# Strassen's scheme for the last two up tiles of each MLP's first block, with the operand sums made behind its first four tiles

## The chip, the cores and the metric

The kernel runs on one core of a Trainium2 chip. The metric is the device time of one execution in microseconds (us); a comparison takes the median of several runs. TensorE (PE) multiplies, VectorE (DVE) and ScalarE (ACT) do elementwise work, GpSimd (POOL) a little of it, and SyncE (SP) issues nearly all transfers.

## The reference, cut to what matters

Four layers run over 512 tokens of width 1024. Each has a mixer (retention, convolution, gated linear attention, retention) and then a squared-ReLU MLP of inner width 4096, with an RMS norm ahead of and behind each part:

```python
def sq_relu_mlp(u, w_up, w_down):
    return jnp.square(jax.nn.relu(u @ w_up)) @ w_down

u = rmsnorm(h, norm_gains[i, 2])
h = h + rmsnorm(sq_relu_mlp(u, mlp_w_up[i], mlp_w_down[i]), norm_gains[i, 3])
```

All of it is float32. The change touches `u @ w_up` alone.

## The kernel before, in words

Everything is stored with features on the 128 partitions and the 512 tokens along the row, so an activation of width 1024 is eight tiles of 128x512. Each float32 operand is cut into a high part (rounded by an ACT copy, L146 or L190 for weights, L435 or L437 for activations) and a low part (the rest, a DVE subtraction, L147, L191, L442, L444), and a product is three matmuls: high by high, high by low, low by high (`mm3`, L454 to L456). PE's order is the order in which the program is written. The order on ACT, DVE and SP is set by a planner that runs through the program with estimated times: an engine that comes free takes, of the instructions whose inputs and buffers are ready by its reckoning, the one that was written first. On the chip each engine then keeps that order.

Weights come as panels of 128x1024 (eight 128x128 blocks, the whole inner width for one output tile). `Stream` loads a panel into a raw buffer and cuts it into a ring of six high and six low buffers. It runs some panels ahead of the matmuls.

An MLP (`mlp`, L683 on) works through four blocks of 1024 inner features: first eight up tiles, each evacuated into `act` by `up` (a ReLU times the norm's factor `r` on DVE, L705; a square on ACT, L706; the two parts on ACT and DVE), and then eight down tiles that add into `y`. Blocks 1 to 3 form the up tiles in pairs with one level of Strassen's scheme (`seven`): a pair is a 2x2 product of halves (four of the eight inner tiles, 256 of the 512 tokens, one of the two output tiles), and takes seven products of 4 x 3 matmuls of 256 columns instead of two tiles of 8 x 3 matmuls of 512. The products are written in the order 1, 2, 5, 6, 4, 3, 7 and use three PSUM banks: `a` for products 1, 6 and 7, `bd` for 2 and 4, `c` for 5 and 3. Two temporaries `e1` and `e2` hold the partial sums that ACT copies out of `a` and `c`. The weight sums that it needs are formed by `pair` (four DVE operations of 128x512, L195 to L200, and three and a half panels cut instead of two). The activation sums (products 3, 5, 6 and 7) are formed once in an MLP by `make(k)`, k from 0 to 3: two ACT scalings (L613, L614), four DVE operations of 128x256 (L615 to L618), and two splits (L435 and L442, tile `wS`). Before the change this is written behind down tiles 2 to 5 of block 0.

Block 0 is formed without the scheme. At the start of an MLP the norm's factor `r` is not known yet, and the second half of the tokens still comes out of the mixer's closing. So `lead` forms up tiles 0 to 3 together, first for tokens 0 to 255 and then for the rest, and keeps their four banks. It then has `norm` write the sum of squares' mean (`mean2`, two matmuls, L285) and the steps to `r` (ACT L461, DVE L467 to L469) into the program once 11.0 us of matmuls, by the program's own count, have gone by after the four tiles. Right behind this it writes the evacuation of the four tiles and of those finished meanwhile. PSUM has eight banks here: seven with the tag `ps` that matmul results share, and one, `st`, for the mean. The temporaries `tmp` (128x512) have four buffers. `make`, `up`, `seven` and the steps to `r` all draw on them.

Of the kernel before, what the change touches and what calls it, by code (L numbers as in the profile page):

```python
# [23 lines left out]
T = 512  # L24
D = 1024
KD = D // P
# [213 lines left out]
def _spare(pool, tag, bufs, w=8 * P):  # L240

    def alloc():
        return [[pool.tile([P, w], F32R, name=f"w{tag}", tag=tag, bufs=bufs) for _ in range(8 * P // w)] for _ in range(2)]
    return alloc
# [98 lines left out]
class Kern:  # L343
# [339 lines left out]
    def mlp(self, close, early=()):  # L683
        nc = self.nc
        FB = 4
        early = list(early)

        def step():

            if early:  # L690
                self.W.cut_early(early.pop(0))

        with self.tc.tile_pool(name="mlp", bufs=1) as mp:
            self.W.keep(FB * 2 * KD - 4, [_spare(mp, "w", 8)] * 4)
            for b in range(1, FB):
                for n in range(0, KD, 2):
                    self.W.pairs[self.W.at + b * 2 * KD + n] = mp
            make = self.combos(mp)
            for b in range(FB):
                act = [self.pair(mp, "act", 2 * KD) for _ in range(KD)]  # L700

                def up(n, ps, c, t=None):
                    lo, hi = c
                    t = self.tmp() if t is None else t
                    nc.vector.scalar_tensor_tensor(t[:, lo:hi], ps[:, lo:hi], 0.0, self.r[:, lo:hi], ALU.max, ALU.mult)  # L705
                    nc.scalar.activation(t[:, lo:hi], t[:, lo:hi], AF.Square)  # L706
                    self.split(act[n], t[:, lo:hi], c)

                n0 = 0
                if b == 0:  # L710
                    n0 = 4
                    self.lead(n0, up)
                if b:
                    for n in range(0, KD, 2):
                        self.seven(lambda i, t: up(n + i, t, (0, T), t))
                    n0 = KD
                for n in range(n0, KD):
                    ps = self.proj()
                    self.when(lambda n=n, ps=ps: up(n, ps, (0, T)))

                def down(n, ps, c):
                    if b == 0:
                        close.first(n, ps)
                    else:
                        close.add(n, ps, c)

                n1 = KD - 4 if b == FB - 1 else KD
                def complete(n, ps):
                    down(n, ps, (0, T))
                    step()  # L730
                    if b == FB - 1:
                        close.done(n)


                for n, ps in enumerate(self.proj2(act)):
                    complete(n, ps)
                for n in range(2, n1):
                    complete(n, self.proj(act))
                    if b == 0 and n < 6:
                        make(n - 2)  # L740
                if n1 < KD:
                    pan = self.W.group(4, 4)
                    self.trail([([pan[i].blk(k) for k in range(KD)], act, n1 + i) for i in range(4)], down, close)
# [1006 lines left out]
```

## Time and profile before

| | us |
|---|---|
| median of 3 runs | 2722.18 (2721.29 to 2722.32) |
| the profiled execution | 2721.62 |
| its span | 2719.9 |
| PE busy | 2671.6 (98%) |
| DVE busy | 1939.8 (71%) |
| ACT busy | 1348.7 (50%) |

The profile is of one execution. The span runs from its first to its last instruction. A matmul's shown duration includes its passage through the array, so the next one starts long before the shown end; what a stream of matmuls costs is the step from one start to the next.

### The profile page before, as it was taken

The page shows a single profiled execution, that of the slowest core. Times are in us where ns is not written, and L with a number is a line of the kernel's source. Part 1 is how long each engine was busy: PE and PEld are TensorE (multiplying, and loading weights), DVE is VectorE, ACT ScalarE, POOL GpSimd, SP SyncE. Part 2 cuts the span into 40 slices and gives each one's busy share as a digit, 9 for nine tenths or more (in the row PEclk, how much of TensorE's full clock was granted, in tenths as well). Part 3 has the DMA queues.
Part 4 walks back from the last instruction along what each step waited for, and adds up shares of the span by engine and source line. Part 5 has one row for each costly group of instructions (what it writes and reads, how often), then busy time and mean ns, then how long its engine had stood idle before and what let it go on. Part 6 is the DMA issues. An engine that isn't in the chain of part 4 may idle for free.

```text
span 2719.9 us, 38414 instructions
## 1 busy us (share of the span) xinstructions
PE 2671.6 (98%) x15232; PEld 2349.5 (86%) x15232; DVE 1939.8 (71%) x3022; ACT 1348.7 (50%) x2098; POOL 180.8 (7%) x183
## 2 busy tenths in 40 slices
PE   9999999999999899999999999999999999999998
PEld 7888889889998898999887888899888888989997
DVE  8755568878859977766788686777765565777766
ACT  5443445655536455544477555455544443555432
POOL 5320000000008400000000000000000000000000
PEclk9999999999999999999999999999999999999999
DMA  5433232676636432332222232333223222223322
GB/s 188 168 132 100 71 100 82 244 268 233 218 124 212 144 112 86 109 117 65 91 70 78 71 109 70 109 109 109 93 63 93 85 70 85 86 86 109 117 63 70
DMA packets 89029, 313.37 MB, mean 115 GB/s; under 512 B 9872, under 2 KB 12176, under 8 KB 88848
## 3 DMA queue, kind: packets, MB, share of 16 engines
q1 hardware_dynamic: 85536, 299.31, 34.4%
q0 software_dynamic: 3168, 11.54, 1.1%
q8 instruction: 119, 1.95, 0.3%
q14 instruction: 62, 0.51, 0.1%
q10 hardware_dynamic: 144, 0.07, 0.0%
HBM read 271.55 MB, written 39.32 MB: 114 GB/s over the span
## 4 chain that ended last, share of the span: by engine, by line
PE 84%; DVE 8%; DMA 3%; ACT 3%; POOL 1%; issue 1%; SPq 0%; DVEq 0%; ACTq 0%
PE ps L455 28%; PE ps L456 28%; PE ps L454 28%; DVE wlo L147 1%; DMA wraw<-in_wst_dram 1%; DMA cuth<-whi 1%; DVE ps L1098 1%; DVE acc L267 1%; ACT whi L146 1%; DVE tmp L329 0%; DMA cutl<-wlo 0%; DVE h L332 0%; PE st L275 0%; DMA h<-in_xT_dram 0%; DVE actl L442 0%
## 5 line engine op out<-in xcount | busy, mean ns | idle before, releaser
L454 PE MATMUL ps<-xh,whi 128*128 128x256 f32 (+1 forms) x1920 | 643.7, 335 | 0.9 <-ACT xh L437 0.9
L455 PE MATMUL ps<-xl,whi 128*128 128x256 f32 (+1 forms) x1920 | 640.1, 333 | 1.1 <-DVE xl L444 1.1
L456 PE MATMUL ps<-xh,wlo 128*128 128x256 f32 (+1 forms) x1920 | 639.5, 333 | 0.0
L146 ACT ACTIVATE whi<-wraw 128x1024 fp32r<-128x1024 f32 (+1 forms) x300 | 312.2, 1045 | 315.2 <-PE ps L455 213.6
L147 DVE TENSOR_TENSOR wlo<-wraw,whi 128x1024 fp32r<-128x1024 f32 (+1 forms) x300 | 365.1, 1220 | 107.5 <-ACT whi L146 105.0
L455 PEld LDWEIGHTS ps<-xl,whi 128*128 128x128 f32 x1920 | 365.3, 190 | 38.7 <-DVE xl L444 1.5
L454 PEld LDWEIGHTS ps<-xh,whi 128*128 128x128 f32 x1920 | 365.2, 190 | 38.1 <-ACT xh L437 1.1
L456 PEld LDWEIGHTS ps<-xh,wlo 128*128 128x128 f32 x1920 | 365.1, 190 | 35.7
L455 PE MATMUL ps<-actl,whi 128*128 128x512 f32 x896 | 350.3, 391 | 3.7 <-DVE actl L442 3.7
L454 PE MATMUL ps<-acth,whi 128*128 128x512 f32 x896 | 349.0, 390 | 0.6 <-ACT acth L435 0.5
L456 PE MATMUL ps<-acth,wlo 128*128 128x512 f32 x896 | 348.7, 389 | 0.0
L308 DVE TENSOR_TENSOR y<-y,ps 128x512 f32<-128x512 f32 (+1 forms) x200 | 114.8, 579 | 216.0 <-PE ps L456 215.3
L454 PE MATMUL ps<-wS,whi 128*128 128x256 f32 x768 | 217.5, 283 | 0.7 <-ACT tmp L654 0.7
L456 PE MATMUL ps<-wS,wlo 128*128 128x256 f32 x768 | 217.3, 283 | 0.0
L455 PE MATMUL ps<-wS,whi 128*128 128x256 f32 x768 | 217.3, 283 | 0.0
L455 PEld LDWEIGHTS ps<-actl,whi 128*128 128x128 f32 x896 | 168.2, 188 | 43.7 <-DVE actl L442 9.4
L454 PEld LDWEIGHTS ps<-acth,whi 128*128 128x128 f32 x896 | 168.2, 188 | 35.9 <-ACT acth L435 1.4
L456 PEld LDWEIGHTS ps<-acth,wlo 128*128 128x128 f32 x896 | 168.2, 188 | 34.6
L190 ACT ACTIVATE whi<-wraw 128x1024 fp32r<-128x1024 f32 x96 | 101.4, 1057 | 142.0 <-PE ps L455 115.6
L190 ACT ACTIVATE whi<-raw 128x1024 fp32r<-128x1024 f32 x96 | 81.2, 845 | 160.0 <-PE ps L455 130.0
L267 DVE TENSOR_TENSOR acc<-acc,sq 128x256 f32<-128x256 f32 (+1 forms) x246 | 121.8, 498 | 51.1 <-ACT sq L266 44.8
L454 PEld LDWEIGHTS ps<-wS,whi 128*128 128x128 f32 x768 | 147.4, 192 | 1.1 <-ACT tmp L654 1.1
(345 smaller groups left out, 5249.0 us busy)
## 6 DMA issues: line engine op xcount, KB each, us to landing
wraw<-in_wst_dram SPq DMA_DIRECT2D x390, 512.0 KB, 3.7
raw<-in_wst_dram SPq DMA_DIRECT2D x48, 512.0 KB, 4.3
cuth<-whi SPq DMA_DIRECT2D x24, 512.0 KB, 3.5
cutl<-wlo SPq DMA_DIRECT2D x24, 512.0 KB, 4.1
whi<-cuth SPq DMA_DIRECT2D x20, 512.0 KB, 3.7
wlo<-cutl SPq DMA_DIRECT2D x20, 512.0 KB, 4.6
diagh<-dg POOLq DMA_DIRECT2D x11, 512.0 KB, 3.2
diagl<-dg POOLq DMA_DIRECT2D x11, 512.0 KB, 3.6
```

Source lines behind the costliest of these rows:

```text
L146: nc.scalar.activation(h, raw[:, c:d], AF.Copy)
L147: nc.vector.tensor_tensor(l, raw[:, c:d], h.bitcast(F32), ALU.subtract)
L190: nc.scalar.activation(hi[0][:, :w], raw[:, :w], AF.Copy)
L267: nc.vector.tensor_tensor(acc, acc, t, ALU.add)
L308: self.K.nc.vector.tensor_tensor(y, y, ps[:, a:b], ALU.add)
L454: mm(out, lhsT=A[0], rhs=B[0], start=start, stop=False)
L455: mm(out, lhsT=A[0], rhs=B[1], start=False, stop=False)
L456: mm(out, lhsT=A[1], rhs=B[0], start=False, stop=stop)
L1098: nc.vector.scalar_tensor_tensor(sums[i], x, w, sums[i], ALU.mult, ALU.add)
```

## The change

The up tiles 6 and 7 of block 0 are formed by `seven` as one pair; tiles 4 and 5 stay as they were. `pair` builds the weight sums for it. The four `make(k)` are written right behind `lead`, ahead of tiles 4 and 5, instead of behind down tiles 2 to 5. Tiles 0 to 3 and blocks 1 to 3 stay. The assertion checks at build time that the pair's panels haven't been loaded as plain ones.

```diff
-            for b in range(1, FB):
-                for n in range(0, KD, 2):
+            for b in range(FB):
+                for n in range(0 if b else KD - 2, KD, 2):
+                    assert self.W.at + b * 2 * KD + n >= self.W.loaded
                     self.W.pairs[self.W.at + b * 2 * KD + n] = mp
...
                 if b == 0:
                     n0 = 4
                     self.lead(n0, up)
-                if b:
-                    for n in range(0, KD, 2):
-                        self.seven(lambda i, t: up(n + i, t, (0, T), t))
-                    n0 = KD
-                for n in range(n0, KD):
-                    ps = self.proj()
-                    self.when(lambda n=n, ps=ps: up(n, ps, (0, T)))
+                    for k in range(4):
+                        make(k)
+                    for n in range(n0, KD - 2):
+                        ps = self.proj()
+                        self.when(lambda n=n, ps=ps: up(n, ps, (0, T)))
+                for n in range(0 if b else KD - 2, KD, 2):
+                    self.seven(lambda i, t: up(n + i, t, (0, T), t))
...
                     complete(n, self.proj(act))
-                    if b == 0 and n < 6:
-                        make(n - 2)
```

## Rows read from the trace of the kernel before

**Rows 1.** The page: span, busy time of three engines, the chain's shares by engine

```profile
span 2719.9 us, 38414 instructions
PE 2671.6 (98%) x15232; PEld 2349.5 (86%) x15232; DVE 1939.8 (71%) x3022; ACT 1348.7 (50%) x2098; POOL 180.8 (7%) x183
PE 84%; DVE 8%; DMA 3%; ACT 3%; POOL 1%; issue 1%; SPq 0%; DVEq 0%; ACTq 0%
```

**Rows 2.** Timeline of PE, first MLP: start us, us, engine, line, operation, tiles [idle before]

```profile
460.33 0.40 PE L454 MATMUL ps<-xh,whi 128*128 128x512 f32 x1
...
471.93 0.62 PE L285 MATMUL st<-sq,onesr 128*128 128x512 f32 x2
472.39 0.40 PE L454 MATMUL ps<-xh,whi 128*128 128x512 f32 x1
...
482.62 0.39 PE L454 MATMUL ps<-acth,whi 128*128 128x512 f32 x1
...
486.93 0.50 PE L455 MATMUL ps<-actl,whi 128*128 128x512 f32 x1 [0.24 <-DVE actl L442]
```

**Rows 3.** Windows (span, busy us of PE, PEld, DVE, ACT, POOL, PEclk, DMA): four pairs

```profile
613.53:653.85 40.32, 40.32 (x338) 40.31 (x336) 36.21 (x51) 27.38 (x44) 0.00 (x0) 1.00 0.53 164
```

**Rows 4.** Timeline of ACT and DVE, first MLP, from the mean to the evacuations

```profile
472.59 0.69 ACT L461 ACTIVATE tmp<-st,eps 128x512 f32<-128x512 f32 x1 [0.32 <-PE st L285]
473.45 0.74 DVE L467 SCALAR_TENSOR_TENSOR tmp<-st,eps,tmp 128x512 f32<-128x512 f32 x1
474.95 0.69 DVE L469 SCALAR_TENSOR_TENSOR rx<-tmp 128x512 f32<-128x512 f32 x1
475.68 2.48 DVE L705 SCALAR_TENSOR_TENSOR tmp<-ps,rx 128x512 f32<-128x512 f32 x4
480.85 1.29 DVE L442 TENSOR_TENSOR actl<-tmp,acth 128x512 fp32r<-128x512 f32 x2
```

**Rows 5.** Timelines of PE and DVE, the same places in the last MLP

```profile
2397.86 0.62 PE L285 MATMUL st<-sq,onesr 128*128 128x512 f32 x2
2401.61 2.49 DVE L705 SCALAR_TENSOR_TENSOR tmp<-ps,rx 128x512 f32<-128x512 f32 x4
```

**Rows 6.** Windows up to the first evacuation, first and last MLP

```profile
455.10:475.70 20.60, 20.60 (x113) 17.93 (x113) 15.39 (x26) 10.64 (x18) 0.00 (x0) 1.00 0.45 137
2381.00:2401.60 20.60, 20.60 (x114) 17.93 (x113) 15.39 (x25) 10.75 (x18) 0.00 (x0) 1.00 0.43 139
```

**Rows 7.** DVE's groups by line, 455.1 to 475.6: xcount | busy, mean ns | idle before

```profile
L147 DVE TENSOR_TENSOR wlo<-wraw,whi 128x1024 fp32r<-128x1024 f32 x6 | 7.3, 1222 | 3.7 <-ACT whi L146 3.7
L267 DVE TENSOR_TENSOR acc<-acc,sq 128x256 f32<-128x256 f32 x14 | 5.8, 422 | 0.6
```

**Rows 8.** DVE's groups by line, 486 to 512, for operations of `make`

```profile
L442 DVE TENSOR_TENSOR wS<-tmp,wS 128x512 fp32r<-128x512 f32 x8 | 5.5, 686 | 0.1
L615 DVE TENSOR_TENSOR tmp<-tmp 128x256 f32<-128x256 f32 x4 | 1.7, 422 | 0.2
```

**Rows 9.** Timeline of DVE: steps from start to start for three sizes

```profile
490.64 0.42 DVE L618 TENSOR_TENSOR tmp<-tmp 128x256 f32<-128x256 f32 x1
490.97 0.42 DVE L617 TENSOR_TENSOR tmp<-tmp 128x256 f32<-128x256 f32 x1
...
509.07 1.22 DVE L191 TENSOR_TENSOR wlo<-raw,whi 128x1024 fp32r<-128x1024 f32 x1
510.21 0.69 DVE L442 TENSOR_TENSOR wS<-tmp,wS 128x512 fp32r<-128x512 f32 x1
510.81 0.69 DVE L195 TENSOR_TENSOR wraw<-wraw,raw 128x512 f32<-128x512 f32 x1
```

**Rows 10.** Timeline of PE: a wait in the third layer's mixer

```profile
1574.82 0.38 PE L454 MATMUL ps<-ogh,whi 128*128 128x256 f32 x1 [2.73 <-ACT ogh L435]
1575.63 0.58 PE L455 MATMUL ps<-ogl,whi 128*128 128x256 f32 x1 [0.43 <-DVE ogl L442]
```

**Rows 11.** Windows: the stretch right behind that wait

```profile
1575.60:1579.00 3.40, 3.37 (x16) 3.37 (x16) 1.33 (x2) 0.63 (x1) 0.00 (x0) 0.50 0.38 140
```

## The prediction

> **What bounds the kernel now.** I read the page first: PE is busy for 98% of the span and carries 84% of the chain of work that ended last, DVE 8% [rows 1]. So PE's stream of matmuls sets the time, and a change counts by the matmul time that it removes and by the gaps that it opens in that stream. Then I read PE's timeline through block 0 of the first MLP. Up tiles 4 to 7 run from 460.33 to 482.62 without a gap, with the mean's two matmuls at 471.93 taking 0.46 of it, and the first small waits stand behind them, at the start of the down tiles, for the low parts of `act` (486.93; with the one before it 0.6 us) [rows 2]. Last I followed DVE and ACT over the same stretch: the mean's result leads by ACT 472.59, DVE 473.45 to 474.95 to the first evacuation at 475.68, four of them back to back [rows 4]. The last MLP has the same distances (mean 2397.86, evacuation 2401.61) [rows 5]; so I work out one MLP and multiply by four.
>
> **What the pair saves.** 96 matmuls of 512 columns take 482.62 - 460.33 - 0.46 = 21.83 us, 0.2274 each [rows 2]. Tiles 6 and 7 are 48 of them: 10.92 us. Four pairs by the scheme took 40.32 us [rows 3], 10.08 a pair (84 matmuls at 0.120). Saved: 0.84 us in an MLP, 3.4 us in all. By the Trainium skill ("TensorE: Matmul & The Clock Gate", section Back-to-back issue gap) a lone matmul's step is its columns at the full clock plus 2.5 ns, and the same section warns that weight loads lengthen it at small widths. By the bare formula the pair would save an estimated 1.2 us; the row has the weight loads in it (PEld busy 40.31 of 40.32) and decides.
>
> **The bank that the pair waits for.** This is what the saving has to be held against. There are seven `ps` banks. Tiles 0 to 3 hold four until the first evacuations, tiles 4 and 5 two, so product 1 takes the seventh, and product 2 (`bd`) must wait for the first evacuation. Before, tile 6 filled the seventh bank for 5.5 us, and the mean, `r` and the evacuation ran behind it. Product 1 lasts 1.44 us. Where does the mean stand? The count of 11.0 us passes 10.36 in tiles 4 and 5 and 0.65 in two steps of product 1 (0.33 each by the program's count); they take 0.72 us, so the mean is again issued at about 471.95. PE then does the other half of product 1, until 471.95 + 0.46 + 0.72 = 473.1. The first evacuation starts at 475.68 and ends 0.7 later, at 476.4 [rows 4]. Wait: 3.3 us, with the chain from mean to evacuation exactly as fast as before. It can't be less unless that chain is shorter, and it has one ACT and four DVE operations in a row. Product 5's bank follows 0.6 us after and costs nothing.
>
> **What delays that chain.** DVE has 20.6 us from the last part of x to the first evacuation and is busy for 15.4 of them: 5.2 idle, in the first MLP as in the last [rows 6]. Six panels' low parts are in it [rows 7]. Steps on DVE, start to start: 0.33 us for 128x256, 0.60 for 128x512, 1.14 for a panel [rows 9]. Written ahead of the mean there are now:
> - four `make`: 16 operations of 128x256 (four lines of four; one of them is shown) and 8 splits of 128x512 [rows 8], 16 x 0.33 + 8 x 0.60 = 10.1 us;
> - the pair's weights: three panels and a half cut, 3 x 1.14 + 0.60 = 4.0, and four sums, 2.4;
> - the first two down panels, 2.3.
> Together 18.8 in place of six panels, 6.8: 12.0 more, against 5.2 idle. If all of it goes first, the chain is 6.8 us later; if the planner lets the chain through, 0 (a gain is excluded, since the mean is not issued sooner). The two down panels wait for ring buffers that tiles 4 and 5 free late, so I leave them behind the chain: 4.5 us. I take this value because the order follows the text of the program, and the mean's split and the steps to `r` are the last written; the products also need most of that work themselves (product 5 all of `make`'s first sums and the second weight panel), so letting the chain through would only move the wait.
>
> ACT takes four times two scalings and two splits, some 9 us, over a stretch where it is busy for 10.6 of 20.6 [rows 6]: it fits. The pair's two raw loads replace two of the same size, issued as early; SP and POOL get nothing more. Taking `make` out of the down tiles frees no PE time there: PE didn't wait for DVE between 487 and the end of the block, so I cost that at 0 (to -0.3).
>
> **Clock.** In the third mixer PE waited 2.73 and 0.43 us, and the granted clock was then 0.50 (1.2 GHz) from 1575.6 to 1579.0 [rows 10, 11]: 16 matmuls of 256 columns in 3.4 us, 0.21 each instead of 0.120, a loss of 1.5 us. A wait of 3.3 to 10 us is as long or longer. Part of the slow stretch may fall into the wait itself, so I take 0.8 in each MLP, with 0 and 1.5 as ends. The Trainium skill says the same of idle gaps ("TensorE: Matmul & The Clock Gate", section Why this matters for your kernels), and by it every one of the four waits would cost a slow stretch, four times 1.5 us by the row.
>
> **Behind the pair.** From the first evacuation DVE has six evacuations (two steps of 0.60 each, 7.2 us), two down panels and a sum, 10 us, while PE does six products (8.6) and the first inner tiles of the down products. The 0.6 us that PE waited at the down tiles goes, since PE comes later by more than the evacuations do: -0.6, with +0.6 as the other end.
>
> **Sum** for an MLP: -0.84 + 3.3 + 4.5 + 0.8 - 0.6 = +7.2 us; four: +29. The profiled execution took 2721.6 us, its span 2719.9; the median of the runs is 2722.2. Forecast: 2751 us. With all ends low the main case is bounded by the next rival; with all high it is -0.84 + 3.3 + 6.8 + 1.5 + 0.6 = 11.4, four times 46: 2768. Its own range is 2738 to 2768.
>
> **Rivals.**
> - The bank's wait alone: the chain keeps its old pace since the planner has room before (5.2 us idle), and only the 3.3 us are paid. -0.84 + 3.3 - 0.6 = 1.9, with the slow clock up to 3.4: 2730 to 2736. For it: in all four MLPs DVE waits for ACT ahead of the chain. Against: 10 us of `make` don't fit into 5.2.
> - Temporaries: four buffers, and `e1` and `e2` want two while six evacuations want one each. If `e1` is served behind them, ACT's copy of product 1 waits until the third evacuation gives its buffer back, which before was at 482.1 [rows 4], 5.7 behind the end of the first one; product 6, which adds into `a`, would be due 2.9 behind it. 3 us more in each MLP, +10.2, four times 41: 2763, up to 2780 with the other ends high. For it: `make` holds three of four just before. Against: the buffers may go in the order in which they were asked for, and `e1` comes first.
> - Not slower: the wait doesn't arise, because the first evacuation ends when product 1 does. Then 0.84 and perhaps 0.6 us are saved in each MLP: 2716 to 2719. It decides at a first evacuation that ends by 473.9, 2.5 us sooner than before. Nothing in the rows gives this: the mean is issued where it was, and the chain behind it has no idle time worth 2.5 us.
>
> **Chances.** Main case 0.57, the bank alone 0.23, temporaries 0.14, not slower 0.06. The range for 8 in 10 runs from 2730 to 2772. About 0.2% (5.4 us) is what a measurement of this kernel tells from no change: the last rival's 3.4 us lie within it for the most part, so faster 0.01, same 0.05, slower 0.94.
>
> **What would show it.** In the changed kernel's PE timeline: a gap ahead of the second product of the pair in block 0 (an x operand, 256 columns, about 1.4 us of matmuls behind tile 5's end) that ends with an evacuation on DVE (L705), in all four MLPs; or, if DVE is late already with the mean's split, part of that gap ahead of L285. The distance from the last x part to the first evacuation grows from 20.6 to about 25, with DVE nearly without idle time in it. The granted clock has four new stretches at 0.5. A pair without a gap would overthrow the forecast; a gap of about 3.3 with DVE as before would be the first rival; a gap ahead of product 6 the second.

## The result and the profile of the changed kernel

The changed kernel takes 2782.0 us (median of 4 runs, 2780.2 to 2787.2) against 2722.3 of the kernel before on the same chip: a ratio of 1.0223, interval 1.0211 to 1.0235. I had forecast 2751 (2730 to 2772): slower was right, but it lost 60 us where I had worked out 29.

The page of the changed kernel, the same three lines as [rows 1]. The shares in its last line add up to 82% and not to 100%, since this chain could be followed back no further than 508.66 us; so its 66% for PE can't be held against the 84% of before.

```profile
span 2785.5 us, 38798 instructions
PE 2692.8 (97%) x15376; PEld 2374.7 (85%) x15376; DVE 1959.9 (70%) x3058; ACT 1361.6 (49%) x2122; POOL 179.1 (6%) x183
PE 66%; DVE 9%; ACT 3%; DMA 3%; issue 1%; SPq 0%; DVEq 0%; ACTq 0%
```

PE's timeline in the first MLP, answering [rows 2]: tile 4's start, the three waits, the first down product and the wait behind it.

```profile
461.96 0.40 PE L454 MATMUL ps<-xh,whi 128*128 128x512 f32 x1
...
479.07 1.70 PE L285 MATMUL st<-sq,onesr 128*128 128x512 f32 x2 [5.33 <-ACT sq L435]
...
484.66 0.55 PE L454 MATMUL ps<-xh,whi 128*128 128x256 f32 x1 [2.61 <-DVE tmp L706]
...
491.78 0.39 PE L454 MATMUL ps<-wS,whi 128*128 128x256 f32 x1 [2.24 <-ACT tmp L654]
...
499.12 0.40 PE L454 MATMUL ps<-acth,whi 128*128 128x512 f32 x1
...
508.70 0.50 PE L455 MATMUL ps<-actl,whi 128*128 128x512 f32 x1 [0.96 <-DVE actl L442]
```

From tile 4 to the first down product it is now 37.16 us; it was 22.28 [rows 2]. The three waits stand ahead of the mean (for the split of the sum of squares), ahead of the pair's second product (for the first evacuation, which gives the bank), and ahead of its fourth, product 6 (for ACT's copy of product 1 into `e1`). Counted from start to start, less a matmul's usual step, they are 5.5, 2.9 and 2.4 us; I count all waits so below. The last MLP [rows 5]; the first two waits are the same in all four to 0.02 us, the third lies between 2.0 and 2.7:

```profile
2455.13 1.70 PE L285 MATMUL st<-sq,onesr 128*128 128x512 f32 x2 [5.33 <-ACT sq L435]
2460.71 0.55 PE L454 MATMUL ps<-xh,whi 128*128 128x256 f32 x1 [2.61 <-DVE tmp L706]
2467.83 0.39 PE L454 MATMUL ps<-wS,whi 128*128 128x256 f32 x1 [2.13 <-ACT tmp L654]
2459.88 2.48 DVE L706 SCALAR_TENSOR_TENSOR tmp<-ps,rx 128x512 f32<-128x512 f32 x4
```

DVE and ACT from the last sum of squares to that copy, answering [rows 4]:

```profile
477.69 0.42 DVE L267 TENSOR_TENSOR acc<-acc,sq 128x256 f32<-128x256 f32 x1
479.23 0.68 DVE L442 TENSOR_TENSOR sq<-acc,sq 128x512 fp32r<-128x512 f32 x1
481.59 0.75 DVE L467 SCALAR_TENSOR_TENSOR tmp<-st,eps,tmp 128x512 f32<-128x512 f32 x1 [1.67 <-ACT tmp L461]
483.82 2.48 DVE L706 SCALAR_TENSOR_TENSOR tmp<-ps,rx 128x512 f32<-128x512 f32 x4
486.39 0.69 DVE L442 TENSOR_TENSOR actl<-tmp,acth 128x512 fp32r<-128x512 f32 x1
487.12 0.69 DVE L706 SCALAR_TENSOR_TENSOR tmp<-ps,rx 128x512 f32<-128x512 f32 x1
...
490.42 2.56 DVE L442 TENSOR_TENSOR actl<-tmp,acth 128x512 fp32r<-128x512 f32 x4
...
484.61 1.23 ACT L707 ACTIVATE tmp<-tmp 128x512 f32<-128x512 f32 x2 [3.05 <-DVE tmp L706]
...
491.38 0.36 ACT L654 ACTIVATE tmp<-ps 128x256 f32<-128x256 f32 x1
```

The copy at 491.38 takes 0.36 us and needs only product 1, whose last matmul started at 481.63 on PE; ACT was idle for 3.05 us up to 484.61 and did not do it. It stands behind the evacuations, since its buffer is one that they give back (`d_own` below shows it). The times fit this: four evacuations run without a gap, the fifth starts (487.12) as the first one's low part of `act` ends (486.39 and 0.69), and the copy follows the third low part, the first of the four from 490.42 on.

Windows of the changed kernel (columns as in [rows 3]). The first answers [rows 6]: it runs from the last part of x, which ends at 457.92 here, to the first evacuation. The second ends with the mean's split, and the last two are the slow stretches behind the waits, answering [rows 11]:

```profile
457.92:483.80 25.88, 18.69 (x98) 15.69 (x96) 24.13 (x47) 17.02 (x30) 0.00 (x0) 0.90 0.31 102
455.10:479.90 24.80, 19.43 (x114) 16.83 (x112) 24.80 (x52) 18.93 (x34) 0.00 (x0) 0.97 0.32 107
478.40:488.60 10.20, 6.81 (x26) 5.94 (x27) 8.17 (x13) 5.30 (x10) 0.00 (x0) 0.50 0.02 8
492.07:495.48 3.41, 3.41 (x18) 3.41 (x18) 0.99 (x3) 1.62 (x4) 0.00 (x0) 0.50 0.37 135
```

From the last part of x to the first evacuation it is 25.9 us where it was 20.6, and I had said about 25. DVE was busy for all of the 24.8 us up to the mean's split. The profiled run is 65.6 us longer than before. Over the four MLPs the mean is late by 4 x 5.5 = 22.0 us; the way from the mean to the first down product grew from 10.68 to 19.64 on average, 35.9; block 0's down products gained 1.9. Another 9.8 us lie elsewhere, all but 0.5 of it ahead of tile 4, in mixers and leads, and the tail gained 0.3. Of the 9.8, 2.5 are waits in the leads for low parts of x (3.4 us in all, 0.9 in the kernel before). They come with the pair: DVE's first weight sum stands ahead of such a part and waited 1.30 us for its raw panel to land.

```profile
441.42 0.69 DVE L195 TENSOR_TENSOR wraw<-wraw,raw 128x512 f32<-128x512 f32 x1 [1.30 <-DMA raw<-in_wst_dram]
442.56 0.39 PE L455 MATMUL ps<-xl,whi 128*128 128x256 f32 x1 [0.78 <-DVE xl L444]
```

All ten kernels here with a pair in block 0 have these waits, 2.8 to 3.5 us in all; the four without one have 0.9. The profiled run was also the slowest of the four, 5 us over the median, and in `d_own` below, with the same code up to the pair, the whole part that is 9.8 here is 1.7; I put no more of it down to the change than those waits.

### The profile page after: what moved, and what is told of

Its sections match the earlier page's. It is cut to its first block, busy times and chain, and to the rows that moved or that the text cites. A ratio compares the mean times of both kernels' runs of the same rounds, so it can differ in the third digit from the quotient of the medians.

```text
span 2785.5 us, 38798 instructions
## 1 busy us (share of the span) xinstructions
PE 2692.8 (97%) x15376; PEld 2374.7 (85%) x15376; DVE 1959.9 (70%) x3058; ACT 1361.6 (49%) x2122; POOL 179.1 (6%) x183
## 4 chain that ended last, share of the span: by engine, by line
PE 66%; DVE 9%; ACT 3%; DMA 3%; issue 1%; SPq 0%; DVEq 0%; ACTq 0%
PE ps L455 22%; PE ps L454 22%; PE ps L456 22%; DMA wraw<-in_wst_dram 2%; DVE wlo L147 1%; DVE acc L267 1%; DVE ps L1097 1%; DVE tmp L329 1%; ACT whi L146 1%; DVE h L332 0%; DVE wS L442 0%; DMA cutl<-wlo 0%; ACT tmp L707 0%; PE st L275 0%; DVE xl L444 0%
## 5 line engine op out<-in xcount | busy, mean ns | idle before, releaser
L454 PE MATMUL ps<-xh,whi 128*128 128x256 f32 (+1 forms) x1904 | 637.3, 335 | 11.4 <-DVE tmp L706 10.5
L456 PE MATMUL ps<-xh,wlo 128*128 128x256 f32 (+1 forms) x1904 | 632.5, 332 | 0.0
L146 ACT ACTIVATE whi<-wraw 128x1024 fp32r<-128x1024 f32 (+1 forms) x292 | 304.2, 1045 | 335.6 <-PE ps L455 234.0
L147 DVE TENSOR_TENSOR wlo<-wraw,whi 128x1024 fp32r<-128x1024 f32 (+1 forms) x292 | 355.9, 1221 | 122.3 <-ACT whi L146 121.2
L454 PE MATMUL ps<-wS,whi 128*128 128x256 f32 x832 | 238.7, 287 | 9.0 <-ACT tmp L654 9.0
L455 PE MATMUL ps<-wS,whi 128*128 128x256 f32 x832 | 238.0, 286 | 0.0
L456 PE MATMUL ps<-wS,wlo 128*128 128x256 f32 x832 | 238.0, 286 | 0.0
L190 ACT ACTIVATE whi<-wraw 128x1024 fp32r<-128x1024 f32 x104 | 109.8, 1056 | 157.5 <-PE ps L455 115.4
L190 ACT ACTIVATE whi<-raw 128x1024 fp32r<-128x1024 f32 x104 | 87.9, 845 | 173.5 <-PE ps L455 128.2
L454 PEld LDWEIGHTS ps<-wS,whi 128*128 128x128 f32 x832 | 162.5, 195 | 10.1 <-ACT tmp L654 10.1
L456 PEld LDWEIGHTS ps<-wS,wlo 128*128 128x128 f32 x832 | 162.4, 195 | 0.0
```

Source lines behind the costliest of these rows:

```text
L146: nc.scalar.activation(h, raw[:, c:d], AF.Copy)
L147: nc.vector.tensor_tensor(l, raw[:, c:d], h.bitcast(F32), ALU.subtract)
L190: nc.scalar.activation(hi[0][:, :w], raw[:, :w], AF.Copy)
L454: mm(out, lhsT=A[0], rhs=B[0], start=start, stop=False)
L455: mm(out, lhsT=A[0], rhs=B[1], start=False, stop=False)
L456: mm(out, lhsT=A[1], rhs=B[0], start=False, stop=stop)
```

## The experiments

My theory after the result: two separate losses, a mean that waits for DVE, and behind it a pair that waits for ACT and DVE (bank, `e1`'s buffer) with a slow clock on top. One table for all kernels, averages over the four MLPs, worked out from PE's timelines, in us ("mean" is its first matmul, "down" the first down product, "both" the way from tile 4 to it; each ratio is to the kernel before, timed beside that run, with its 95% interval):

```
           time (median)   ratio to before    tile 4 to mean   mean to down   both
before       2722.3                              11.60            10.68       22.28
after        2782.0     1.0223 [1.0211,1.0235]   17.11            19.64       36.75
a_make       2751.0     1.0109 [1.0092,1.0126]   17.33            13.22       30.55
b_pair       2759.9     1.0142 [1.0127,1.0157]   11.62            19.03       30.65
c_fill       2777.7     1.0205 [1.0190,1.0220]   17.14            18.68       35.81
d_own        2770.4     1.0182 [1.0167,1.0197]   17.11            16.74       33.86
e_half       2738.8     1.0061 [1.0047,1.0075]   14.29            13.38       27.67
f_nor        2721.4     0.9998 [0.9989,1.0006]   11.60            11.07       22.67
g_nor        2786.1     1.0234 [1.0220,1.0248]   13.03            24.85       37.88
h_late       2809.4     1.0317 [1.0299,1.0334]   11.62            32.58       44.20
i_pool       2783.4     1.0226 [1.0210,1.0241]   19.32            17.79       37.11
b_own        2756.0     1.0122 [1.0107,1.0137]   11.62            16.68       28.30
j_pair       2735.1     1.0045 [1.0031,1.0059]   13.03            12.27       25.30
k_fill       2775.8     1.0192 [1.0178,1.0206]   17.22            16.55       33.77
```

### a_make and b_pair: each half alone

```
a_make, from before:   behind self.lead(n0, up):  for k in range(4): make(k)
                       not behind down tiles 2 to 5; no pair in block 0
b_pair, from after:    makes behind down tiles 2 to 5, as before; in block 0
                       self.S = {i: S[(1, 2, 4)[i % 3]] for i in range(1, 8)}
                       (halves of x take the place of the sums, which are left out)
```

> The operand sums are written behind the first four tiles, as in the change, but block 0 keeps plain tiles 6 and 7. Theory (waits add up: the mean's input late by the sums, the bank, the buffer of e1, and the slow clock behind them): the sums of squares still end late, so PE waits 3.5 to 5.5 us ahead of the mean in each MLP and loses 1.5 to 3 to the clock; no bank wait, since tile 7 comes 5 us later. +20 to +32 us in all, 2742 to 2754. Rival (the bank alone is the root, the sums fit into idle time): 2722 to 2726.

> The pair stands in block 0, but its products 3, 5, 6 and 7 there read halves of x instead of the sums (the result of these two tiles is left wrong), and the sums stay behind the down tiles as before. Theory: mean on time, the bank waits 3.3 us in each MLP, product 6 waits some 2.4 for the copy into e1, the clock costs 1.5 to 3, less 0.84 and 0.6: +18 to +32 us, 2740 to 2754. Rival (the sums are the root): at most 2722.

PE's timelines, `a_make` first, then `b_pair`:

```profile
477.60 1.70 PE L285 MATMUL st<-sq,onesr 128*128 128x512 f32 x2 [5.36 <-ACT sq L435]
```

```profile
473.10 0.62 PE L285 MATMUL st<-sq,onesr 128*128 128x512 f32 x2
477.67 0.36 PE L454 MATMUL ps<-xh,whi 128*128 128x256 f32 x1 [3.23 <-DVE tmp L706]
484.73 0.39 PE L454 MATMUL ps<-xh,whi 128*128 128x256 f32 x1 [2.46 <-ACT tmp L654]
```

The waits separate. The makes alone give the whole wait ahead of the mean and no other; the pair alone has its mean on time and both waits behind it. `a_make` came out as expected. `b_pair` lost 38 us, over both expectations, so I had the pair's part too small a second time. In the stretch of the table the two halves lose alike, 8.3 and 8.4 us in each MLP; most of what sets their times apart lies ahead of tile 4, 2 us of it in the waits for low parts of x that `a_make` doesn't have. 29.4 + 38.3 is 8 more than the change's 59.8, so the two overlap: behind the mean the makes alone cost 2.5 us in each MLP (13.22 against 10.68), and beside the pair's waits they add only 0.6 (19.64 against 19.03).

### c_fill, d_own and k_fill: the slow clock and e1's buffer

```
c_fill:  46, 24 and 20 extra matmuls of 256 columns, into unused halves of banks,
         in the three waits of the changed kernel
d_own:   e1 = own.tile([P, T], F32, name="e", tag="e", bufs=1)   (block 0's pair)
k_fill:  d_own with the 46 and 24 extra matmuls
```

> The change, with matmuls of no use (256 columns, into unused halves of banks) in the three waits of each MLP: 46 ahead of the mean (5.5 us), 24 ahead of product 2 (2.9), 20 ahead of product 6 (2.4). The waits stay as long, but PE is busy in them. Theory: the granted clock stays full and 4.7 us an MLP come back: 2763 (2758 to 2768). Rival (as forecast, the clock costs 0.8 an MLP): 2779.

> The change, with a buffer of its own for e1 in block 0's pair, outside the four temporaries. Theory: ACT copies product 1 out before the evacuations, the wait ahead of product 6 goes (2.4 us an MLP) and the second slow stretch with it (up to 1.5): 10 to 16 us less than the change, 2766 to 2772. Rival (that wait is ACT's own queue, or another takes its place): no different from the change, 2780 to 2784.

> d_own (the changed kernel with a buffer of its own for e1) with filler matmuls in the two waits that are left, 46 ahead of the mean and 24 ahead of the pair's second product. In c_fill the same fillers brought only 4 us, with e1's buffer still shared. Theory (the slow clock costs where no later wait hides it: of d_own's slow stretch of 10 to 13.7 us in each MLP, some 8 us lie on work, at half the speed): 3 to 4 us in each MLP come back, 2754 to 2760 us. Rival (the slow stretch costs as little as in c_fill, 1 us in each MLP): 2765 us or more.

PE's timeline of `c_fill` (L667 are the extra matmuls); a window of its last MLP; lines of PE and ACT of `d_own`, then of `k_fill`:

```profile
473.69 5.68 PE L667 MATMUL ps<-xh,onesr 128*128 128x256 f32 x46
...
484.48 0.36 PE L455 MATMUL ps<-xh,whi 128*128 128x256 f32 x1 [0.31 <-DVE tmp L721]
487.42 2.56 PE L667 MATMUL ps<-xh,onesr 128*128 128x256 f32 x20
491.61 0.39 PE L455 MATMUL ps<-wS,whi 128*128 128x256 f32 x1 [1.63 <-ACT tmp L658]
```

```profile
2458.80:2462.20 3.40, 3.40 (x17) 3.40 (x18) 0.96 (x2) 1.50 (x3) 0.00 (x0) 0.50 0.01 5
```

```profile
484.14 0.55 PE L454 MATMUL ps<-xh,whi 128*128 128x256 f32 x1 [2.61 <-DVE tmp L706]
481.56 0.38 ACT L654 ACTIVATE e<-ps 128x256 f32<-128x256 f32 x1 [0.53 <-PE ps L456]
```

```profile
491.65 0.39 PE L455 MATMUL ps<-wS,whi 128*128 128x256 f32 x1 [1.83 <-ACT tmp L658]
489.25 1.04 ACT L146 ACTIVATE whi<-wraw 128x1024 fp32r<-128x1024 f32 x1
```

`d_own` went as expected: with a buffer of its own the copy into `e1` runs at 481.56, ahead of the evacuations, the wait ahead of product 6 is gone, and 11.6 us, 2.9 in each MLP, come back. A smaller wait of 0.5 to 0.8 us takes its place ahead of product 3 in three MLPs.

In `c_fill` the order on ACT and DVE is that of the changed kernel. In three MLPs the granted clock was 1.00 throughout the stretch, and product 6 still started at 491.61, where it started at 491.78 with the slow clock: the copy sets it, not PE. Only some 4 us came back, 1 in each MLP, as the rival had it: 1.8, 0.3 and 1.7 in these three, and 0.1 in the last, where a stretch at 0.50 followed product 6's wait. So in the changed kernel the way from the mean to the down tiles is paced by evacuations and copies on ACT and DVE; how fast PE runs between hardly counts.

`k_fill` was to show what the clock costs with the wait for `e1` out of the way, and the theory failed: mean to down is 16.55 against 16.74, and the wait ahead of product 3 is now 2.0 to 2.5 us, again for a copy on ACT (L658, the changed kernel's L654). But the extra matmuls also changed the planner's order on ACT: a panel's split (489.25) went ahead of the copy that this product waits for, and `e1`'s copy behind the first evacuations. So `k_fill` doesn't part the clock from that order, and what the clock costs in `d_own` stays open. Its total is 5 us above `d_own`, from waits outside this stretch (the block-1 tiles and the second mixer); I have no explanation for those.

### e_half, h_late and i_pool: time on DVE, or order

```
e_half, from before:  make(0), make(1) behind the lead tiles; make(2), make(3) as before
h_late, from after:   for k in range(4): self.when(lambda k=k: make(k))
                      behind tiles 4 and 5
i_pool, from d_own:   in make(k), 4 x  nc.vector.tensor_tensor -> nc.gpsimd.tensor_tensor
```

> The kernel before with only the first two of the four makes moved behind the block's first four tiles; the other two stay behind down tiles 4 and 5, and there is no pair in the first block. Theory A (VectorE only runs out of time: the makes take what idle time it has, and what does not fit delays the sums of squares): two makes are some 5.1 us of VectorE (half of 10.2 us), and VectorE had 5.2 us idle ahead of the mean (rows 6), so the wait ahead of the mean is 1 us or less in each MLP and the run is 2722 to 2730 us. Theory B (any make between the sums of squares breaks their chain, through the order of the queue and the two buffers of the squares): the wait is 2.5 to 3 us in each MLP, half of the 5.5 us that four makes give, with a slow stretch of the clock behind it, and the run is 2733 to 2740 us.

> The changed kernel with its four makes put behind the evacuations that wait for the mean, instead of behind the first four tiles. Theory A (the makes' 10.2 us of VectorE have no free place between the first four tiles and the first down tile; moving them only moves the wait): the mean is on time again (11.6 us behind the fifth tile's start instead of 17.1), the bank wait is about 3.4 us as in b_pair, and the pair's products that read the sums wait for the makes, which start some 13 us behind the mean: the first down tile starts 36 to 42 us behind the fifth tile, against 37.2 in the changed kernel, 2775 to 2800 us. Theory B (what costs is that makes stand among the sums of squares, and elsewhere they fit): the wait on the sums stays under 3 us in each MLP, and the run is 2755 to 2765 us, as b_pair, which has no makes ahead of the pair.

> d_own (the changed kernel with a buffer of its own for e1) with the four additions and subtractions of each make on GpSimd, which is idle there, and the splits left on VectorE: VectorE gets 16 x 0.34 = 5.4 us less in each MLP. GpSimd's rows of before: 1.44 us for a sum of 128x512, so an estimated 0.7 us for 128x256 and some 11 us for sixteen of them. Theory A (VectorE's time is short): the wait ahead of the mean falls from 5.5 to about the 3.2 us of e_half, which adds as much work to VectorE; the bank's wait of 2.9 us stays: 2755 to 2763 us. Theory B (the order matters and not the amount): the wait ahead of the mean stays at 5 us or more, 2768 us or more.

`e_half`, PE's mean and ACT ahead of it:

```profile
475.76 0.51 PE L285 MATMUL st<-sq,onesr 128*128 128x512 f32 x1 [3.03 <-ACT sq L435]
...
466.13 1.06 ACT L146 ACTIVATE whi<-wraw 128x1024 fp32r<-128x1024 f32 x1 [1.53 <-DMA wraw<-in_wst_dram]
468.33 1.06 ACT L146 ACTIVATE whi<-wraw 128x1024 fp32r<-128x1024 f32 x1 [0.52 <-DMA wraw<-in_wst_dram]
...
471.87 1.06 ACT L146 ACTIVATE whi<-wraw 128x1024 fp32r<-128x1024 f32 x1 [1.86 <-PE ps L455]
472.83 0.70 ACT L266 ACTIVATE sq<-h 128x256 f32<-128x256 f32 x2
```

The last squares of the kernel before, on ACT:

```profile
467.17 0.71 ACT L266 ACTIVATE sq<-h 128x256 f32<-128x256 f32 x2
```

Theory A is wrong here. Half of the makes would fit into DVE's 5.2 idle us, and DVE is still idle for some 3 of the 20.6 us from 455.10 to 475.70; yet the mean is 3 us late in three MLPs (1.2 and 0.9 in the other). The squares (L266) stand in ACT's queue behind splits of weight panels (L146), as some did before, and these wait for a load (1.53, 0.52) and for PE to give a buffer back (1.86). Here the last squares stand behind all three of these splits and start at 472.83; in the kernel before they started at 467.17. So a part of the loss is order. With four makes and the pair DVE has no idle time left; with four makes alone (`a_make`) it is idle for 1.7 of 24.2 us, and the mean is as late.

`h_late` shows that from the other side. PE's timeline:

```profile
473.82 0.62 PE L285 MATMUL st<-sq,onesr 128*128 128x512 f32 x2
478.39 0.36 PE L454 MATMUL ps<-xh,whi 128*128 128x256 f32 x1 [3.23 <-DVE tmp L706]
488.56 0.55 PE L454 MATMUL ps<-wS,whi 128*128 128x256 f32 x1 [7.62 <-issue]
491.64 0.58 PE L454 MATMUL ps<-wS,whi 128*128 128x256 f32 x1 [1.61 <-ACT wS L435]
```

The mean is on time and the pair waits 7.6 us for the first sums and again for each further one: 44 us from tile 4 to down, more than my range of 36 to 42. Theory A, in the direction, and beyond it in size. Between the lead and the first down tile there is no free place for the makes.

`i_pool` took the sums off DVE and made the mean later still, 19.3. That is theory B's number, but not for B's reason. DVE's group that adds the squares, from 455 to 483, in `d_own`, then in `i_pool`, then GpSimd's groups of `i_pool`:

```profile
L267 DVE TENSOR_TENSOR acc<-acc,sq 128x256 f32<-128x256 f32 x14 | 5.8, 422 | 0.0
```

```profile
L267 DVE TENSOR_TENSOR acc<-acc,sq 128x256 f32<-128x256 f32 x14 | 9.7, 697 | 0.7 <-ACT wS L435 0.5
...
L618 POOL TENSOR_TENSOR tmp<-tmp 128x256 f32<-128x256 f32 x16 | 18.9, 1182 | 0.0
L616 POOL TENSOR_TENSOR tmp<-tmp 128x256 f32<-128x256 f32 x16 | 13.9, 866 | 1.3
```

The same sum went from 422 to 697 ns on average, and GpSimd's own took 0.87 to 1.18 us over the whole run. Of the fourteen, the five with no GpSimd sum beside them took 0.42 us each, the other nine 0.85 on average. The Trainium skill ("SBUF — State Buffer", section SBUF: two separate sides) says that a VectorE operation with two inputs in SBUF and a GpSimd operation exclude each other for a whole instruction; the trace agrees, with its 0.42 and 0.85 us. So `i_pool` does not tell A from B.

### f_nor, g_nor, b_own and j_pair: the evacuations out of the way

```
f_nor, block 0:  t = relu(ps), square   instead of   t = relu(ps) * r, square
                 (the ReLU on ACT, each tile's written as the tile ends)
                 y = ps * r2 at the first down product; r2 = r * r
g_nor:   the changed kernel with the same edit
j_pair:  f_nor with the pair of b_pair
b_own:   b_pair with d_own's buffer
```

> The kernel before, without makes moved and without a pair in the first block; the first block's activation is made without the factor r (ScalarE takes the Relu and the square straight from the bank), and the first down product is multiplied by r squared on VectorE instead. The evacuations of the first four tiles then wait for no mean. It is the base for the run g_nor. Theory: nothing that the path waits for changes ahead of the down tiles, and the stall ahead of the first down tile (0.58 us in each MLP) may go: 2718 to 2723 us. If ScalarE's larger share of the evacuations makes the act tiles later, the wait ahead of the first down tile grows, to 2724 to 2730 us.

> The changed kernel with the first block's activation made without the factor r, as in f_nor. Banks and temporaries of the first four tiles then come free as each tile ends, and neither the bank for the pair's second product nor the buffer for its copy hangs on the mean. Theory: of the waits of 5.5, 2.9 and 2.4 us in each MLP, the last two go altogether; the first goes too if the mean may be late without anyone waiting at TensorE, but the mean's matmul stands in TensorE's own order, so it keeps up to 5.5 us unless the sums of squares come earlier: 2740 to 2748 us with that wait, 2714 to 2722 us if it goes too. If the sums for the pair are late (about 10 us of makes behind the evacuations), the wait moves to the product that reads them and the run is 2750 us or more.

> b_pair (the pair in the first block on halves of x in place of the sums, the makes where they were before) with a buffer of its own for e1: only the bank's wait is left of what the evacuations cost the pair. Theory (bank and temporary each cost what their wait shows): of b_pair's +38 us, the e1 wait of 2.5 us in each MLP and a part of the slow clock behind it go, and the bank's 3.4 us stays, less the pair's 0.84: 2743 to 2752 us. Rival (the two waits cover each other, and the next use of a bank or temporary takes the place): 2755 us or more.

> f_nor (the first block's activation without the factor r; 0.9998 of before) with the pair in the first block, on halves of x in place of the sums, and the makes where they were before: the pair alone, with the banks and temporaries of the first four tiles free before it starts and no make ahead of it. Theory (the pair is worth its 0.84 us in each MLP once nothing of the change's surroundings holds it): the first down tile starts some 0.8 us earlier than in f_nor (21.5 to 22.0 us behind the fifth tile), and the time is 2717 to 2720 us. Rival (the pair brings a wait of its own, whoever holds the banks: its evacuation ends with e2, e1 and two splits right ahead of the down tiles, and its weights are needed as sums early): the first down tile starts at 23.5 us or later, and the time is 2726 us or more.

`f_nor` is level with before: when tiles 6 and 7 are plain, the evacuations' wait for the mean costs nothing. In `b_own` the wait ahead of product 6 is gone and others came in its place. PE's timeline, 48 matmuls (products 2, 5, 6 and 4) behind product 2's start at 478.42:

```profile
486.44 0.39 PE L454 MATMUL ps<-xh,whi 128*128 128x256 f32 x1 [0.62 <-ACT tmp L654]
```

This is product 3, which waits for ACT's copy of product 5 into `e2`; that copy too stands behind the evacuations. The first MLP adds up: 22.28 - 0.84 + 3.4 for the bank + 0.8 ahead of product 3 + 1.7 (a slow stretch of 3.4 us at half speed) = 27.3, measured 27.17; in the other three 1.4 to 2.2 us come ahead of product 3, and in all four 0.8 to 2.9 us at the start of the down tiles for `act`. So the rival's time came true (2756.0): the next copies and `act` took the place.

`g_nor` missed its cheap cases; its last one came true. Its bank and `e1` waits are gone; the wait moved to the pair's products that read the sums, 1.2 to 3.0 us at a time, since the makes now stand behind the evacuations; its mean is late by 1.4 us too. `j_pair`, with no make ahead and no bank held, is the pair alone, and it loses 12 us. PE's mean in `j_pair`, and ACT ahead of it:

```profile
474.77 0.49 PE L285 MATMUL st<-sq,onesr 128*128 128x512 f32 x1 [1.25 <-ACT sq L435]
476.26 0.50 PE L285 MATMUL st<-sq,onesr 128*128 128x512 f32 x1 [0.99 <-DVE sq L442]
...
472.62 1.06 ACT L146 ACTIVATE whi<-wraw 128x1024 fp32r<-128x1024 f32 x1
...
474.11 0.61 ACT L435 ACTIVATE sq<-acc 128x512 fp32r<-128x512 f32 x1
```

Even alone, the pair has a mean that waits twice (1.4 and 1.2 us, with a slow stretch behind it in three MLPs). The sum of squares ends at 472.13 (DVE, 471.71 and 0.42), but ACT's part of its split starts at 474.11, behind a panel's split and a part of an evacuation, and DVE's part comes later still. The rival's numbers came true (23.5 us or later, 2726 us or more), but by another wait than it named: down starts 25.3 us behind tile 4, 2.6 us later than in `f_nor`, by a wait at the mean. No kernel here beat the one before.

## Why the prediction was wrong

- **The pair's saving, -0.84.** Not contradicted (the sum for `b_own` holds with it), but never seen by itself.
- **The bank, +3.3.** Right: 3.38 us where the mean is on time (`b_pair`, `h_late`), 2.9 in the changed kernel.
- **The chain to the mean, +4.5.** Right in place, 5.5 in size, inside the bounds of 0 and 6.8. I left the two down panels, 2.3, behind the chain; they went ahead of it (two operations of L147, at 471.83 and 473.94, lie among the 24.8 busy us). And I counted four weight sums there; two of them, 1.2 us, run at 441.42 and 443.49, before that stretch. With both put right my sum gives 4.5 + 2.3 - 1.2 = 5.6. I also had the split of the sum last in an otherwise punctual chain: the sums of squares themselves end late, at 478.1.
- **The clock, +0.8.** There were slow stretches behind all four means, as I expected. The rule of the Trainium skill that I quoted ("TensorE: Matmul & The Clock Gate", section Why this matters for your kernels) holds for their presence, 10.2 to 13.7 us long at 0.50; three of the four shorter waits ahead of product 6, 2.3 to 2.7 us, had one of 3.4 us as well. The cost in the time is 1 us in each MLP (`c_fill`), since the next wait hides the rest.
- **Behind the pair, -0.6.** -1.9 us in all four MLPs where I had -2.4.
- **The step that failed** is that nothing stands between the bank's wait and the down tiles: "Product 5's bank follows 0.6 us after and costs nothing", and the copies into `e1` and `e2` at no cost in the main sum. From mean to down I had +3.3 us (-0.84 + 3.3 + 0.8); it was +9.0, four times 5.7 too little: 23 us of the profiled run's miss of 37. `d_own` shows a half of it: the temporary, 2.9 us in each MLP, at the place and nearly the price that my second rival gave (3 us, product 6, `e1` served behind the evacuations). I gave it 0.14, because `e1` is asked for first in the text. But in the program the evacuations stand where the mean is issued, in the middle of product 1, ahead of the copy into `e1`; so they had the four buffers first, and in the trace the copy follows the third one's release. The other half no run isolates. In `d_own`'s timelines it consists of the mean's second matmul waiting for its split (0.7 us), the slow clock (2.8 us behind the mean where I had 0.8) and 0.5 us ahead of product 3, less 0.4 by which the bank's wait was shorter than I had it.
- **The other misses**: 4 us from the chain, and some 9.5 us of the profiled run outside the stretch. Of these some 5 are that run's own, and 2.5 are the waits in the leads: I had the pair's raw loads as early enough to cost nothing, and DVE waited for them.

What stays open: how the chain's 5.5 us divide between DVE's time and the order of squares behind weight panels, what the slow clock costs once `e1` has its own buffer, and the waits of `k_fill` outside the stretch.

## What to carry to other kernels

When a wait moves ahead of a burst of evacuations, price everything that is queued behind that burst: banks, then temporaries, then in-order copies on ACT; taking one wait away here gave back only what the next did not claim (`b_own`, `c_fill`). Idle time on an engine is no free place for work whose position in the queue delays something due (5.1 us of makes in 5.2 us of idle time cost 3 us). And a transformation that saves 0.84 us of PE must be asked first whether its operands can be made anywhere at all.

## What the runs showed of the hardware

- Matmuls that kept the granted clock at 1.00 through the waits (`c_fill`, in three of the four stretches) gave back 4 us in all, though the changed kernel ran 13.6 us of each stretch at 0.50 (1.2 GHz): slow matmuls between two waits that other engines end cost some 1 us in each.
- GpSimd sums beside VectorE sums slowed VectorE's: 0.42 us alone, 0.85 beside them. GpSimd's own took 0.87 to 1.18 us for 128x256, where I had estimated 0.7 from a row of 128x512.
- VectorE keeps its order through a late load: a weight sum that waited 1.30 us for its panel held back a part of x behind it, and TensorE waited 0.78 us for that part.
